# S5 input products of a hybrid decoder layer: split float32r operands stacked through DRAM, or plain float32 on four 32-row blocks

## The chip, the cores and the metric

The program runs on one NeuronCore of a Trainium2 chip. The metric is the time of one execution on the device in microseconds (us), the median of several runs. The engines are TensorE (PE; its weight loads are listed apart as PEld), VectorE (DVE), ScalarE (ACT), GpSimd (POOL) and SyncE (SP). Each works through its own instructions in the order in which the program lists them and waits on semaphores for the others.

## What is computed

One decoder layer on 256 positions of width 2048: RMSNorm, one wide projection, three mixing branches (gated MLP, S5 state-space model, stick-breaking attention), their gated sum, an output projection, and an MLP of 8192. The change is in the S5 branch. Its 1024 channels form 64 groups of 16, and each group drives 64 complex states:

```python
u = xin.astype(f32).reshape(bsz, seq, S5_GROUPS, S5_GROUP_CH)
bu_re = jnp.einsum('blgh,gph->blgp', u, bb_re)
bu_im = jnp.einsum('blgh,gph->blgp', u, bb_im)
_, _, s_re, s_im = lax.associative_scan(combine, (a_re, a_im, bu_re, bu_im), axis=1)
y = einsum('blgp,ghp->blgh', s_re, c_re) - einsum('blgp,ghp->blgh', s_im, c_im)
```

The input products are `bu_re` and `bu_im`. The kernel puts the factor that turns `b` into `bb` into the output weights instead, so the products use `b` as it is loaded.

## The kernel before

**The stream.** Almost all work is in large matmuls over weight blocks of 512 KB, numbered in the order in which they are used (`plan`): S5 input (blocks 0 to 15), q, k and v (16 to 63), the MLP branch's v and u (64 to 95), gates and branch outputs (96 to 223), the GLU (from 224), and so on. Each block is loaded into a `raw` tile by SP's queue (L195), cast to `hi` in float32r by ScalarE (L214), and the rest `lo` = raw - hi is taken by VectorE. `begin_unit(u)` loads five blocks ahead and converts three ahead; then PE does the block's matmuls with hi and lo (L289 and L293, or L351, L352 and L354, or L320, L321 and L328).

**The side work.** Everything else is in tasks, generators that `pump()` (L224) advances once after each block. A task that yields BAR goes on after the next block; a budget of VectorE time per block, which all tasks share, can end its turn earlier. New tasks go to the front of the list unless `front=False`. So attention and the gated MLP come ahead of S5 wherever both are ready, and a task that emits less VectorE work lets those behind it come earlier. The instructions of a task stand on each engine behind those of the block after which they were emitted.

**Side results.** Products of the tasks go to PSUM tiles `side(name)` (L141), from the pool `ps_sd` of four banks. A bank is free for a new tile when the last instruction that reads the old one is done. Attention uses two such tiles for each step of a pair of heads: `pz` (scores), `pc` (sums of logs), `pyc` (output). Their names carry the head: `pc6` and `pc7` belong to the pair whose other tiles are `za3`, `le3` and `sp3`. `le` takes the sums by an addition on VectorE and then an exponential on ScalarE (L882). The gated MLP's task `gmlp` (L911) opens with the row sums `rv_s` on VectorE, from the sums of squares `ssv` of `vg`.

**S5.** A half h is 128 channels, that is four row blocks of 32 channels with 128 states each; a chunk ch is half of it (two row blocks, j). `s5_split_b` (L513) loads `b` in two tiles, splits each into hi and lo and stores both in the DRAM tile `bd`; `s5_split_u` (L529) does the same with the S5 input `s5x` into `ud`. For each chunk `stack` (L653) reads back three pieces for each operand, so that 96 rows hold hi, lo, hi of `b` against hi, hi, lo of `u`: one float32r matmul over 96 rows then is the product. `bu_mm` (L668) does four of these a chunk into two side tiles `pb`, and `bu_evac` (L678) copies them to `bu` on ScalarE. Then VectorE rotates `bu` by a table `cs` (products `rt`, made from table products `tt`), scans, rotates back, and `y_mm` (L767) forms the output `py`, in float32, with eight matmuls on four blocks of columns. `s5_go` (L996) starts this when the preparation and the splits are done. Small tiles of 128x1024 float32 come from one pool of `NACT` = 32.

Of the kernel before, what the change touches and what calls it, by code (L numbers as in the profile page):

```python
# [17 lines left out]
P = 128  # L18
D = 2048
T = 256  # L20
# [7 lines left out]
NACT = 32  # L28
# [63 lines left out]
def hybrid_trunk(  # L92
# [31 lines left out]
    dram = ctx.enter_context(tc.tile_pool(name="dram", bufs=1, space=bass.MemoryType.DRAM))  # L124
# [384 lines left out]
    ud = dram.tile([P, MT, 2, T], F32R, name="ud")  # L509
    bd = dram.tile([P, MT, 2, 2 * P], F32R, name="bd")  # L510
    st = {}

    def s5_split_b():  # L513

        for i in range(2):
            br = a4([P, 4, 2 * P], F32, f"br{i}")
            S.dma_start(br, s5_b[:, 4 * i:4 * i + 4])
            yield BAR
            yield BAR
            hi = a4([P, 4, 2 * P], F32R, f"bh{i}")  # L520
            lo = a4([P, 4, 2 * P], F32R, f"bl{i}")
            S.copy(hi, br)
            V.tensor_sub(lo, br, hi.bitcast(F32))
            yield 1135
            yield BAR
            G.dma_start(bd[:, 4 * i:4 * i + 4, 0, :], hi)
            G.dma_start(bd[:, 4 * i:4 * i + 4, 1, :], lo)

    def s5_split_u(i):  # L529
        hi = a4([P, 4, T], F32R, f"uh{i}")  # L530
        lo = a4([P, 4, T], F32R, f"ul{i}")
        S.copy(hi, s5x[i])
        V.tensor_sub(lo, s5x[i], hi.bitcast(F32))
        yield 1135
        yield BAR
        G.dma_start(ud[:, 4 * i:4 * i + 4, 0, :], hi)
        G.dma_start(ud[:, 4 * i:4 * i + 4, 1, :], lo)
# [109 lines left out]
    def s5_run():  # L647
        mag, kre, kim, e1, e16, e128 = (st[n] for n in ("mag", "kre", "kim", "e1", "e16", "e128"))
        bu_of, cks, cts, st_of, bs_of, tab, py, pbs, tmp = {}, {}, {}, {}, {}, {}, {}, {}, {}
        bdv = bd.rearrange("(i p) h s c -> p h s i c", p=32)  # L650
        udv = ud.rearrange("(i p) h s c -> p h s i c", p=32)

        def stack(ch):  # L653

            h, c = divmod(ch, 2)
            bs = s5w.tile([P, 2, 2 * P], F32R, tag="bs", name=f"bs{ch}")
            su = s5w.tile([P, 2, T], F32R, tag="su", name=f"su{ch}")
            for blk in range(3):
                rows = slice(32 * blk, 32 * blk + 32)
                G.dma_start(bs[rows], bdv[:, h, blk % 2, 2 * c:2 * c + 2])  # L660
                G.dma_start(su[rows], udv[:, h, blk // 2, 2 * c:2 * c + 2])
            bs_of[ch], st_of[ch] = bs, su
            if c == 1:
                ct = s5w.tile([P, 2, 4, 32], F32, tag="ct", name=f"ct{h}", bufs=1)
                S.dma_start(ct, s5_c[:, h])
                cts[h] = ct
# [11 lines left out]
        def bu_evac(ch):  # L678
            bu = a4([P, 2, 2, T], F32, f"bu{ch}")
            for j, pb in enumerate(pbs.pop(ch)):  # L680
                S.copy(bu[:, :, j, :], pb.rearrange("p (r t) -> p r t", r=2))  # L681
            bu_of[ch] = bu
# [100 lines left out]
        stack(0)  # L783
        yield from table_a(0)
        yield BAR
        stack(1)
# [6 lines left out]
        for ch in range(16):  # L793
            yield BAR
            if ch + 2 < 16:
                stack(ch + 2)
            if ch + 1 < 16:
                bu_mm(ch + 1)
# [3 lines left out]
            if ch + 1 < 16:  # L802
                bu_evac(ch + 1)
# [165 lines left out]
    def do_proj(kind, i, us):  # L969
        dsts = {"s5": s5x, "q": qT, "k": kT, "u": uT}[kind]  # L970

        def ev(b, ps):
            if dsts[i] is None:
                dsts[i] = a4([P, 4, T], F32, f"{kind}{i}")
            dst = dsts[i]
            o = dst[:, 2 * b:2 * b + 2, :]
            V.tensor_mul(o, ps if kind == "s5" else wide_sum(ps, f"w{kind}{i}_{b}"), rb)
            if kind == "u":
                def act():
                    S.activation(o, o, AF.Gelu_apprx_tanh)  # L980
                    if i == 1 and b == 1:
                        gm["u"] = True

                later(1, act)
            if kind == "s5" and b == 1:
                spawn(f"su{i}", s5_split_u(i))
                if i == 1:
                    spawn("s5", s5_go(), front=False)

        if kind == "s5":  # L990
            run_T(us, xs, ev)
        else:
            for j, u in enumerate(us):
                run_W([(u, lambda ps, j=j: ev(j, ps))], xs)

    def s5_go():  # L996
        while any(n in ("s5p", "s5b", "su0", "su1") for n, _ in tasks):
            yield BAR
        for _ in range(3):
# [158 lines left out]
    for kind, arg, us in plan:  # L1158
        if kind == "s5" and arg == 0:
# [3 lines left out]
            def ev0(b, ps):  # L1163
                V.tensor_mul(s5x[0][:, 2 * b:2 * b + 2, :], ps, rb)
                if b == 1:
                    spawn("su0", s5_split_u(0))

            def mid0(i):
# [11 lines left out]
                if i == 7:  # L1180
                    spawn("s5b", s5_split_b(), front=False)
# [93 lines left out]
```

## Time and profile before

| | |
|---|---|
| median of 3 runs | 1545.67 us (1545.59 to 1545.78) |
| the profiled execution | 1545.78 us |
| its span, first to last instruction | 1544.1 us |
| PE busy | 1528.4 us, 99% |
| VectorE busy | 1097.1 us, 71% |
| ScalarE busy | 764.0 us, 49% |
| `pb` matmuls (L674) | 64 records |
| `py` matmuls (L772) | 128 records for 64 matmuls |

A row of the timeline gives the start from the beginning of the span, the time until the last of the row's instructions ends, the engine, the line, the operation, what is written and read, and how many instructions the row joins. Matmuls are pipelined: one that is listed with 390 ns may let the next start after 230, so costs in the stream of PE are read from starts. Square brackets hold the idle time ahead of the row and what ended it.

### The profile page before, as it was taken

To read this page: it belongs to the slowest core of one execution; us is meant where nothing else is said; L and a number is where in the kernel's file an instruction comes from. 1 tells how busy PE (TensorE), PEld (TensorE's weight loads), DVE (VectorE), ACT (ScalarE), POOL (GpSimd) and SP (SyncE) were. 2 spreads that over 40 slices of the span, in tenths; PEclk is the share of its full clock that TensorE was granted. 3 is DMA by queue.
4 is the path that set the end of the run, shared out by engine and by line. 5 is a ranking of instruction groups with operands and counts; after the bars stand their busy time and mean duration, and the time that the engine had idled before them with its cause. 6 is when DMAs were issued, how large, how long until landed. Compare 5 with 4: busy or idle time off the path is not lost.

```text
span 1544.1 us, 20755 instructions
## 1 busy us (share of the span) xinstructions
PE 1528.4 (99%) x7900; PEld 1303.8 (84%) x7900; DVE 1097.1 (71%) x1454; ACT 764.0 (49%) x947; POOL 67.3 (4%) x126
## 2 busy tenths in 40 slices
PE   9999999999999999999999999999999999999997
PEld 9988888888888888898888888888888888888886
DVE  6886988989999999967655665466545564556554
ACT  7546577555546555564444443344434444344442
POOL 0301021001001000000000000000000000000000
PEclk9999999999999999999999999999999999999999
DMA  9965565657666666656666555555555555555653
GB/s 342 328 199 164 186 211 172 197 175 225 202 212 212 199 215 200 192 177 209 205 202 194 188 189 193 196 187 188 192 195 191 188 188 193 195 190 187 219 194 105
DMA packets 97411, 308.67 MB, mean 200 GB/s; under 512 B 11296, under 2 KB 22560, under 8 KB 97312
## 3 DMA queue, kind: packets, MB, share of 16 engines
q1 hardware_dynamic: 79200, 285.25, 56.2%
q0 software_dynamic: 11904, 10.49, 3.2%
q10 hardware_dynamic: 6208, 11.61, 2.4%
q8 instruction: 62, 1.02, 0.3%
q14 instruction: 37, 0.30, 0.1%
HBM read 301.02 MB, written 6.29 MB: 199 GB/s over the span
## 4 chain that ended last, share of the span: by engine, by line
PE 96%; DVE 1%; issue 1%; ACT 1%; DMA 1%; SPq 0%; POOLq 0%; POOL 0%; DVEq 0%; ACTq 0%
PE mm L289 21%; PE mm L351 19%; PE mm L352 19%; PE mm L354 19%; PE mm L293 11%; PE mm L320 1%; PE mm L321 1%; PE mm L328 1%; PE py L772 1%; PE pb L674 0%; DMA raw<-in_w_in 0%; ACT hi L214 0%; DVE lo L86 0%; DMA raw<-in_w_m 0%; DVE x L86 0%
## 5 line engine op out<-in xcount | busy, mean ns | idle before, releaser
L86 DVE TENSOR_TENSOR lo<-raw,hi 128x1024 fp32r<-128x1024 f32 (+1 forms) x537 | 653.3, 1220 | 380.1 <-ACT hi L214 365.5
L214 ACT CAST hi<-raw 128x1024 fp32r<-128x1024 f32 (+1 forms) x537 | 561.4, 1049 | 634.7 <-PE mm L352 397.7
L289 PE MATMUL mm<-xz,hi 128*128 128x512 f32 x1024 | 256.5, 392 | 0.0
L289 PEld LDWEIGHTS mm<-xz,hi 128*128 128x128 f32 x1024 | 184.4, 189 | 33.2
L351 PE MATMUL mm<-hi,xs 128*128 128x512 f32 x512 | 200.8, 392 | 0.0
L352 PE MATMUL mm<-hi,xs 128*128 128x512 f32 x512 | 199.5, 390 | 0.0
L352 PE MATMUL mm<-hi,ff 128*128 128x512 f32 x480 | 186.8, 389 | 0.0
L351 PE MATMUL mm<-hi,ff 128*128 128x512 f32 x480 | 186.8, 389 | 0.0
L293 PEld LDWEIGHTS mm<-xz,lo 128*128 128x128 f32 x1024 | 139.7, 190 | 10.0
L293 PE MATMUL mm<-xz,lo 128*128 128x256 f32 x1024 | 142.8, 282 | 0.0
L354 PE MATMUL mm<-lo,xs 128*128 128x512 f32 x512 | 137.0, 389 | 0.0
L354 PE MATMUL mm<-lo,ff 128*128 128x512 f32 x480 | 128.3, 389 | 0.0
L351 PEld LDWEIGHTS mm<-hi,xs 128*128 128x128 f32 x512 | 96.1, 188 | 21.9 <-ACT bu L681 1.6
L354 PEld LDWEIGHTS mm<-lo,xs 128*128 128x128 f32 x512 | 96.1, 188 | 20.2
L352 PEld LDWEIGHTS mm<-hi,xs 128*128 128x128 f32 x512 | 96.2, 188 | 19.4
L352 PEld LDWEIGHTS mm<-hi,ff 128*128 128x128 f32 x480 | 90.1, 188 | 18.7
L354 PEld LDWEIGHTS mm<-lo,ff 128*128 128x128 f32 x480 | 90.1, 188 | 18.7
L351 PEld LDWEIGHTS mm<-hi,ff 128*128 128x128 f32 x480 | 90.1, 188 | 18.6
L289 PE MATMUL mm<-xs,hi 128*128 128x512 f32 x384 | 96.6, 393 | 0.3 <-DVE s5x L86 0.3
L289 PEld LDWEIGHTS mm<-xs,hi 128*128 128x128 f32 x384 | 69.1, 189 | 13.3 <-ACT hi L214 0.5
L86 DVE TENSOR_TENSOR rt<-bu,cs 128x1024 f32<-128x1024 f32 x64 | 76.8, 1221 | 0.3
L293 PEld LDWEIGHTS mm<-xs,lo 128*128 128x128 f32 x384 | 52.4, 190 | 3.8
(252 smaller groups left out, 1681.3 us busy)
## 6 DMA issues: line engine op xcount, KB each, us to landing
raw<-in_w_m SPq DMA_DIRECT2D x256, 512.0 KB, 4.3
raw<-in_w_in SPq DMA_DIRECT2D x143, 512.0 KB, 4.2
raw<-in_w_wide SPq DMA_DIRECT2D x48, 512.0 KB, 4.4
raw<-in_w_br SPq DMA_DIRECT2D x48, 512.0 KB, 4.3
raw<-in_w_out SPq DMA_DIRECT2D x32, 512.0 KB, 3.8
x<-in_x ACTq DMA_DIRECT2D x8, 512.0 KB, 5.8
raw<-in_w_glu SPq DMA_DIRECT2D x8, 512.0 KB, 4.3
bs<-bd POOLq DMA_DIRECT2D x48, 64.0 KB, 4.7
```

Of the source, the lines that this page charges most:

```text
L86: return fn(*a, **kw)
L214: S.copy(hi[:, k, :], raw[:, k, :])
L289: PE.matmul(pt[:, nb, :], lhsT=hi[:, k, nb * P:(nb + 1) * P], rhs=src.both(4 * i + k), start=4 * i + k == 0, stop=False)
L293: PE.matmul(pt[:, nb, T:], lhsT=lo[:, k, nb * P:(nb + 1) * P], rhs=src.hi(4 * i + k), start=False, stop=4 * i + k == last)
L320: PE.matmul(po, lhsT=wh, rhs=src.hi(kt), start=kt == 0 and nb % 2 == 0, stop=False)
L321: PE.matmul(po, lhsT=wh, rhs=src.lo(kt), start=False, stop=False)
L328: PE.matmul(po, lhsT=lo[:, k, nb * P:(nb + 1) * P], rhs=src.hi(kt), start=False, stop=kt == 2 * nk - 1 and nb % 2 == 1)
L351: PE.matmul(ps[tt], lhsT=xh, rhs=hi[:, k, :], start=kt == 0, stop=False)
L352: PE.matmul(ps[tt], lhsT=xl, rhs=hi[:, k, :], start=False, stop=False)
L354: PE.matmul(ps[tt], lhsT=xh, rhs=lo[:, k, :], start=False, stop=kt == 2 * nk - 1)
L772: PE.matmul(py[h][32 * i:32 * i + 32, :T], lhsT=cks[h][:, ri, i, :], rhs=s[i // 2][:, ri, i % 2, :], start=ri == 0, stop=ri == 1, tile_pos ...
```

## The change

The products are made in plain float32 from the tiles that are there, and the DRAM tiles, the splits and the stacking go. `b` is loaded once into two tiles that stay (`s5_load_b`). For a half, four row blocks i stand at partitions 32i to 32i + 31 of `s5x` and of `b`; each gets matmuls of its own at row position 32i of the array, into a side tile of its own, first the four for the real part, then the four for the imaginary part. So a whole half (two chunks) is done at once, every second chunk. `NACT` is 34, and `s5_go` waits for the preparation alone.

```diff
-NACT = 32
+NACT = 34
...
-        while any(n in ("s5p", "s5b", "su0", "su1") for n, _ in tasks):
-            yield BAR
-        for _ in range(3):
+        while any(n == "s5p" for n, _ in tasks):
             yield BAR
...
+    def s5_load_b():
+        for i in range(2):
+            t = a4([P, 4, 2 * P], F32, f"s5b{i}")
+            S.dma_start(t, s5_b[:, 4 * i:4 * i + 4])
+            s5bs.append(t)
...
-        def bu_mm(ch):
-            su, bs = st_of.pop(ch), bs_of.pop(ch)
-            pbs[ch] = []
-            for j in range(2):
-                pb = side(f"pb{ch}_{j}")
-                for ri in range(2):
-                    PE.matmul(pb[:, ri * T:(ri + 1) * T], lhsT=bs[0:96, j, ri * P:(ri + 1) * P],
-                              rhs=su[0:96, j, :], start=True, stop=True)
-                pbs[ch].append(pb)
+        def bu_mm(h):
+
+            pbs[h] = [side(f"pb{h}_{i}") for i in range(4)]
+            for ri in range(2):
+                for i in range(4):
+                    r = slice(32 * i, 32 * i + 32)
+                    PE.matmul(pbs[h][i][:, ri * T:(ri + 1) * T],
+                              lhsT=s5bs[h // 4][r, h % 4, ri * P:(ri + 1) * P],
+                              rhs=s5x[h // 4][r, h % 4, :], start=True, stop=True,
+                              tile_position=(32 * i, 0))
...
-            if ch + 2 < 16:
-                stack(ch + 2)
-            if ch + 1 < 16:
-                bu_mm(ch + 1)
+            if ch % 2 == 1 and ch < 15:
+                load_c(ch // 2 + 1)
+                bu_mm(ch // 2 + 1)
             if ch > 0 and ch % 2 == 0:
                 y_mm(ch // 2 - 1)
             yield BAR
-            if ch + 1 < 16:
-                bu_evac(ch + 1)
+            if ch % 2 == 1 and ch < 15:
+                bu_evac(ch // 2 + 1)
```

Because the budget of `pump()` is shared, the order of the side work changes too. Three places follow, as they stand on their engines. In these rows the number behind a tile's second underscore is the tile's own, a bracket names the engines that the instruction waits for, and line numbers below belong to the changed file (L839 there is L873 before, L640 is the new `bu_mm`).

PE behind block 79, before: the two `pc` of attention's last pair, then block 80.

```order
L873 MATMUL pc6_2639<-sp3_2550,ntri_119 128x256 [waits DVE_49,PE_49]
L875 MATMUL pc6_2639<-sp3_2550,nones_117 128x128
L876 MATMUL pc6_2639<-sp3_2550,ntri_119 128x128
L873 MATMUL pc7_2643<-sp3_2550,ntri_119 128x256 [waits PE_49]
L875 MATMUL pc7_2643<-sp3_2550,nones_117 128x128
L876 MATMUL pc7_2643<-sp3_2550,ntri_119 128x128
L289 MATMUL mm80_2656<-xs0_145,hi80_2583 128x512 [waits Activation_49]
```

The same place now, from `pc7` on:

```order
L839 MATMUL pc7_2586<-sp3_2493,ntri_117 128x256 [waits PE_49]
L841 MATMUL pc7_2586<-sp3_2493,nones_115 128x128
L842 MATMUL pc7_2586<-sp3_2493,ntri_117 128x128
L640 MATMUL pb2_0_2592<-s5x0_139,s5b0_428 128x256
L640 MATMUL pb2_1_2593<-s5x0_139,s5b0_428 128x256 [waits PE_49]
L640 MATMUL pb2_2_2594<-s5x0_139,s5b0_428 128x256 [waits DVE_49]
L640 MATMUL pb2_3_2595<-s5x0_139,s5b0_428 128x256 [waits DVE_49]
L640 MATMUL pb2_0_2592<-s5x0_139,s5b0_428 128x256
L640 MATMUL pb2_1_2593<-s5x0_139,s5b0_428 128x256
L640 MATMUL pb2_2_2594<-s5x0_139,s5b0_428 128x256
L640 MATMUL pb2_3_2595<-s5x0_139,s5b0_428 128x256
L288 MATMUL mm80_2604<-xs0_141,hi80_2528 128x512 [waits Activation_49]
```

The third group of products (half 2) has come between `pc7` and block 80, and two of its four tiles wait for VectorE.

VectorE at blocks 79 and 80 (lo82 and lo83 are converted three blocks ahead), before:

```order
L86 TENSOR_TENSOR lo82_2624<-raw82_2581,hi82_2623 128x1024 [waits DMAHW4_49,PE_49,Activation_49]
L86 TENSOR_TENSOR cu1_1_2648<-ct1_2132,s5_kre_961 128x256 [waits DVE_49]
L86 TENSOR_TENSOR cu2_1_2649<-ct1_2132,s5_kim_962 128x256
L86 TENSOR_TENSOR ck1_2647<-cu1_1_2648,cu2_1_2649 128x128 [waits DVE_49]
L86 SCALAR_TENSOR_TENSOR ck1_2647<-cu1_1_2648,cu2_1_2649 128x128
L86 SCALAR_TENSOR_TENSOR cs3_2462<-cs3_2462,s5_cs_758,td3_2554 128x128 x2
L86 TENSOR_TENSOR lo83_2660<-raw83_2601,hi83_2659 128x1024 [waits DMAHW5_49,PE_49,Activation_49]
L86 TENSOR_REDUCE rv_s_2685<-ssv_135 128x2 [waits Activation_49]
L86 TENSOR_SCALAR rv_s_2685<-rv_s_2685 128x2 [waits DVE_49]
L86 TENSOR_TENSOR le3_2517<-pc6_2639,za3_2516 128x384 [waits PE_49]
L86 TENSOR_TENSOR le3_2517<-pc7_2643,za3_2516 128x384 [waits PE_49]
```

And now:

```order
L86 TENSOR_TENSOR lo82_2567<-raw82_2526,hi82_2566 128x1024 [waits DMAHW4_49,PE_49,Activation_49]
L86 TENSOR_TENSOR lo83_2608<-raw83_2546,hi83_2607 128x1024 [waits DMAHW5_49,PE_49,Activation_49]
L86 TENSOR_REDUCE rv_s_2633<-ssv_133 128x2 [waits Activation_49]
L86 TENSOR_SCALAR rv_s_2633<-rv_s_2633 128x2 [waits DVE_49]
L86 TENSOR_TENSOR le3_2464<-pc6_2582,za3_2463 128x384 [waits PE_49]
L86 TENSOR_TENSOR le3_2464<-pc7_2586,za3_2463 128x384 [waits PE_49]
```

The S5 rows between lo82 and lo83 have moved to earlier blocks; the additions that read `pc6` and `pc7` stay behind lo83 and `rv_s`.

VectorE ahead of the first pair's additions to `le0` (blocks 45 and 46), before:

```order
L86 SCALAR_TENSOR_TENSOR sp0_1533<-za0_1501,le0_1502 128x768 [waits Pool_49]
L86 SCALAR_TENSOR_TENSOR za0_1501<-za0_1501,le0_1502 128x768 [waits DVE_49]
L86 TENSOR_TENSOR lo48_1624<-raw48_1537,hi48_1623 128x1024 [waits DMAHW6_49,PE_49,Activation_49]
L86 SCALAR_TENSOR_TENSOR cs0_1567<-cs0_1567,s5_cs_758,td0_1616 128x128 x4
L86 TENSOR_TENSOR lo49_1664<-raw49_1577,hi49_1663 128x1024 [waits DMAHW7_49,PE_49,Activation_49]
L86 TENSOR_TENSOR le0_1502<-pc0_1643,za0_1501 128x384 [waits DVE_49,PE_49]
L86 TENSOR_TENSOR le0_1502<-pc1_1647,za0_1501 128x384 [waits PE_49]
```

And now, behind `sp0`, `za0` and the first product `rt1`:

```order
L86 TENSOR_TENSOR rt2_1600<-bu0_1541,cs0_1385 128x1024
L86 TENSOR_TENSOR bu0_1541<-rt1_1599,rt2_1600 128x512 [waits DVE_49]
L86 TENSOR_TENSOR bu0_1541<-rt1_1599,rt2_1600 128x512
L86 TENSOR_TENSOR lo48_1608<-raw48_1547,hi48_1607 128x1024 [waits DMAHW7_49,PE_49,Activation_49]
L86 TENSOR_TENSOR tt1_1_1636<-e16_872,e1_871 128x256 [waits DVE_49]
L86 TENSOR_TENSOR tt2_1_1637<-e16_872,e1_871 128x256
L86 TENSOR_TENSOR tt1_1_1636<-e16_872,e1_871 128x256
L86 TENSOR_TENSOR tt2_1_1637<-e16_872,e1_871 128x256
L86 TENSOR_TENSOR cs1_1635<-tt1_1_1636,tt2_1_1637 128x2x128 [waits DVE_49]
L86 TENSOR_TENSOR cs1_1635<-tt1_1_1636,tt2_1_1637 128x2x128
L86 TENSOR_TENSOR lo49_1647<-raw49_1570,hi49_1646 128x1024 [waits DMAHW0_49,PE_49,Activation_49]
L86 TENSOR_TENSOR le0_1490<-pc0_1627,za0_1489 128x384 [waits PE_49]
```

The S5 chain starts some four blocks earlier (`pb0` stands behind block 41 instead of block 45), so the first rotation and the second table now stand between `sp0` and `le0`. The `pyc` of that pair, which need `le0`, stand behind block 48 instead of block 47.

## Rows read from the trace of the kernel before

**Rows 1.** The page, part 1: busy us of each engine, share of the span, instructions.
```profile
PE 1528.4 (99%) x7900; PEld 1303.8 (84%) x7900; DVE 1097.1 (71%) x1454; ACT 764.0 (49%) x947; POOL 67.3 (4%) x126
```
**Rows 2.** Waits of PE: us in total, times, longest us.
```profile
PE pc L873 <- DVE sp L86: 1.7, 1, 1.7
```
**Rows 3.** Timeline of ScalarE at hi of block 10: start us, us, engine, line, operation.
```profile
29.38 1.05 ACT L214 CAST hi<-raw 128x1024 fp32r<-128x1024 f32 x1 [0.83 <-DMA raw<-in_w_in]
```
**Rows 4.** Timeline of PE, first matmul of block 10.
```profile
36.29 0.28 PE L320 MATMUL mm<-xs,hi 128*128 128x256 f32 x1
```
**Rows 5.** Timeline of PE around a `pb` group that stands alone.
```profile
192.93 1.08 PE L354 MATMUL mm<-lo,xs 128*128 128x512 f32 x4
193.85 0.64 PE L674 MATMUL pb<-su,bs 96*128 96x256 f32 x4
194.32 0.40 PE L351 MATMUL mm<-hi,xs 128*128 128x512 f32 x1
```
**Rows 6.** Timeline of PE around a `py` group that stands alone.
```profile
660.13 1.07 PE L354 MATMUL mm<-lo,xs 128*128 128x512 f32 x4
661.13 1.07 PE L772 MATMUL py<-bu,ck 128*32 128x256 f32 x16
662.13 0.50 PE L351 MATMUL mm<-hi,xs 128*128 128x512 f32 x1
```
**Rows 7.** Timeline of PE behind block 79: `pc6` begins, block 80 begins.
```profile
250.86 0.59 PE L873 MATMUL pc<-sp,ntri 128*128 128x256 f32 x2
...
252.53 2.10 PE L289 MATMUL mm<-xs,hi 128*128 128x512 f32 x8
```
**Rows 8.** Timeline of ScalarE there: hi83, and the last sum of squares of `vg1`.
```profile
250.15 1.06 ACT L214 CAST hi<-raw 128x1024 fp32r<-128x1024 f32 x1 [1.67 <-DVE za L86]
...
255.26 0.18 ACT L391 ACTIVATION_READ_ACCUMULATOR mm<-vg 128x1 f32 x1
```
**Rows 9.** Timeline of VectorE there: `rv_s` and the additions to `le3`.
```profile
256.41 0.15 DVE L86 TENSOR_REDUCE rv_s<-ssv 128x2 f32<-128x4 f32 x1
...
256.67 1.01 DVE L86 TENSOR_TENSOR le<-pc,za 128x384 f32<-128x384 f32 x2
```
**Rows 10.** Timeline of PE at the first `pc` (behind block 45), and blocks 46 and 47.
```profile
141.01 0.70 PE L873 MATMUL pc<-sp,ntri 128*128 128x256 f32 x2 [1.73 <-DVE sp L86]
...
143.35 2.00 PE L289 MATMUL mm<-xs,hi 128*128 128x512 f32 x8
...
146.13 2.00 PE L289 MATMUL mm<-xs,hi 128*128 128x512 f32 x8
```
**Rows 11.** Timeline of VectorE ahead of it: the first table, and `sp0`.
```profile
135.41 1.42 DVE L86 TENSOR_TENSOR tt<-e,e 128x256 f32<-128x256 f32 x4
136.87 0.76 DVE L86 TENSOR_TENSOR cs<-tt,tt 128x256 f32<-128x256 f32 x2
...
140.00 0.95 DVE L86 SCALAR_TENSOR_TENSOR sp<-za,le 128x768 f32<-128x768 f32 x1
```
**Rows 12.** Timeline of ScalarE there: hi46, `le0`'s exponential, copies of `pb`.
```profile
133.20 1.03 ACT L214 CAST hi<-raw 128x1024 fp32r<-128x1024 f32 x1
...
146.28 1.28 ACT L882 ACT_TABLE_LOAD   x1 [5.45 <-DVE le L86]
147.57 0.85 ACT L882 ACTIVATE le<-le 128x768 f32<-128x768 f32 x1
148.32 1.06 ACT L681 COPY bu<-pb 128x512 f32<-128x512 f32 x2
```
**Rows 13.** The page, part 5, VectorE's products: count | busy us, mean ns | idle.
```profile
L86 DVE TENSOR_TENSOR rt<-bu,cs 128x1024 f32<-128x1024 f32 x64 | 76.8, 1221 | 0.3
```
**Rows 14.** Timeline of PE's weight loads in a `pb` group.
```profile
221.81 0.54 PEld L674 LDWEIGHTS pb<-su,bs 96*128 96x128 f32 x4
```
**Rows 15.** Windows behind the last matmul: length, busy us (instructions) of PE, PEld, DVE, ACT, POOL, granted clock, DMA share, GB/s.
```profile
1533.00:1537.00 4.00, 0.00 (x0) 0.00 (x0) 2.58 (x7) 0.51 (x2) 0.56 (x1) 1.00 0.23 87
1537.00:1539.00 2.00, 0.00 (x0) 0.00 (x0) 0.00 (x0) 0.00 (x0) 0.00 (x0) 0.66 1.04 321
```

More of the change, by code (lines that the diff above doesn't have):

```diff
@@ L123, in hybrid_trunk @@
     s5w = ctx.enter_context(tc.tile_pool(name="s5w", bufs=2))
-    dram = ctx.enter_context(tc.tile_pool(name="dram", bufs=1, space=bass.MemoryType.DRAM))
     ps_mm = ctx.enter_context(tc.tile_pool(name="ps_mm", bufs=2, space=bass.MemoryType.PSUM))
@@ L508, in hybrid_trunk @@
     gs = Split(env, MT, "gs")
-    ud = dram.tile([P, MT, 2, T], F32R, name="ud")
-    bd = dram.tile([P, MT, 2, 2 * P], F32R, name="bd")
     st = {}
-    def s5_split_b():
+    s5bs = []
+    def s5_load_b():
         for i in range(2):
-            br = a4([P, 4, 2 * P], F32, f"br{i}")
-            S.dma_start(br, s5_b[:, 4 * i:4 * i + 4])
-            yield BAR
[L519 to L537, printed above, removed]
+            t = a4([P, 4, 2 * P], F32, f"s5b{i}")
+            S.dma_start(t, s5_b[:, 4 * i:4 * i + 4])
+            s5bs.append(t)
     def dve_exp(dst, src, name):
@@ L648, in s5_run @@
         mag, kre, kim, e1, e16, e128 = (st[n] for n in ("mag", "kre", "kim", "e1", "e16", "e128"))
[L649 to L666, printed above, removed]
@@ L668, in bu_mm @@
-        def bu_mm(ch):
-            su, bs = st_of.pop(ch), bs_of.pop(ch)
-            pbs[ch] = []
-            for j in range(2):
-                pb = side(f"pb{ch}_{j}")
-                for ri in range(2):
-                    PE.matmul(pb[:, ri * T:(ri + 1) * T], lhsT=bs[0:96, j, ri * P:(ri + 1) * P],
-                              rhs=su[0:96, j, :], start=True, stop=True)
-                pbs[ch].append(pb)
[L678 to L682, printed above, removed]
+        bu_of, cks, cts, tab, py, pbs, tmp = {}, {}, {}, {}, {}, {}, {}
@@ new lines, in load_c @@
+        def load_c(h):
+            cts[h] = s5w.tile([P, 2, 4, 32], F32, tag="ct", name=f"ct{h}", bufs=1)
+            S.dma_start(cts[h], s5_c[:, h])
+        def bu_mm(h):
[7 more added lines that the diff above has]
+                              tile_position=(32 * i, 0))
@@ L684, in make_ck, with bu_evac @@
+        def bu_evac(h):
+            pb = pbs.pop(h)
+            for c in range(2):
+                bu = bu_of[2 * h + c] = a4([P, 2, 2, T], F32, f"bu{2 * h + c}")
+                for j in range(2):
+                    S.copy(bu[:, :, j, :], pb[2 * c + j].rearrange("p (r t) -> p r t", r=2))
         def make_ck(h):
@@ L781, in y_evac @@
             yield 0
-        stack(0)
+        load_c(0)
         yield from table_a(0)
         yield BAR
-        stack(1)
         table_b(0)
@@ L984, in ev @@
                 later(1, act)
[L985 to L988, printed above, removed]
+            if kind == "s5" and b == 1 and i == 1:
+                spawn("s5", s5_go(), front=False)
         if kind == "s5":
@@ L996, in s5_go @@
     def s5_go():
-        while any(n in ("s5p", "s5b", "su0", "su1") for n, _ in tasks):
-            yield BAR
-        for _ in range(3):
+        while any(n == "s5p" for n, _ in tasks):
             yield BAR
@@ L1164, in ev0 @@
                 V.tensor_mul(s5x[0][:, 2 * b:2 * b + 2, :], ps, rb)
-                if b == 1:
-                    spawn("su0", s5_split_u(0))
             def mid0(i):
@@ L1180, in mid0 @@
                 if i == 7:
-                    spawn("s5b", s5_split_b(), front=False)
+                    s5_load_b()
                     spawn("s5p", s5_prep(), front=False)
```

## The prediction

> **What bounds the kernel now.** Start with the busy times: TensorE (PE) is busy 1528.4 of 1544.1 us [rows 1], VectorE 1097.1, ScalarE 764.0. Next ask whether the rest of PE's time is waits: the longest in its list is one of `pc` on VectorE, 1.7 us [rows 2]; most of what is left lies behind its last matmul. So from the first weight block to the last the program is one stream of matmuls, and a change is worth what it adds to or takes from that stream: time that its own matmuls hold the array, and new waits of PE. The profiled execution took 1545.78 us (span 1544.1 plus 1.68 around it), 0.11 above the median of 1545.67; sums are made on the former and the 0.11 is taken off at the end. One run of this kernel tells 0.2% (3.1 us) from no change; that is the bound for the chances.
>
> **What the removed work gives back.** Four casts on ScalarE, four subtractions on VectorE and, on POOL's queue, eight stores to DRAM and 96 reads back fall away. PE waited for none of them. The casts of block 10 show the cover: hi is ready at 29.38 + 1.05 = 30.43 [rows 3], PE uses it at 36.29 [rows 4], 5.9 us later. The only load that comes earlier, `s5b1`, 0.5 MB beside `s5b0` on ScalarE's queue, starts near the same place and is covered by the same 5.9 us. I cost all of this at nothing.
>
> **What the matmuls cost in the stream.** A `pb` group of before (one chunk) is read from starts: the last of four lo matmuls starts at 192.93 + (1.08 - 0.39) = 193.62, the next thing 0.23 later; with `pb` the next block starts at 194.32 instead of 193.85 [rows 5]. So 0.47 us a chunk, 16 chunks: 7.5 us go.
>
> The new group (a half, two chunks) has eight float32 matmuls on four blocks of the array. No row shows blocks of rows, but `py` is the same count and size on four blocks of columns: 16 records for eight matmuls, two passes each. Undisturbed, the block behind it starts at 662.13, where 660.13 + 0.68 + 0.23 = 661.04 would have been normal [rows 6]: 1.09 us, four rounds of four passes at 0.22 and about 0.1 us of emptying on either side. I take that: 8 x 1.09 = 8.7, so +1.2 us. The nearest rows for the bounds: passes that stream like the float32r `pb`, 0.12 each, give 4 x 0.12 + 0.18 = 0.65 a group (5.2, -2.3 us); passes that do not overlap at all give 16 x 0.22 + 0.18 = 3.7 a group (29.6, +22.1 us).
>
> A rule to set beside this: the Trainium skill (TensorE: Matmul & The Clock Gate, "Measured speedup vs the span model") gives four row blocks 3.07 times the speed of one, not four times. By it 16 passes of 0.22 would take an estimated 1.15 us plus the emptying, and the sum would be about 2 us higher; no run here shows it yet.
>
> **The new wait.** Every new group takes four `side` tiles at once, and `side` has four banks. So PE can't start the group until every earlier side product is read out. In seven of the eight places that has long happened. At block 79 it hasn't: the order puts `pb2` right behind `pc6` and `pc7`, whose banks are freed by the two VectorE additions to `le3`, and these stand one block later, behind lo83 and `rv_s`. PE must wait for them before it can go on to block 80.
>
> When are they done? In the trace of before `pc6` starts at 250.86 and block 80 at 252.53 [rows 7]. `rv_s` needs the sums of squares of `vg1`, which ScalarE makes after hi83 (250.15), with a table load, until 255.26 + 0.18 = 255.44 [rows 8]. All of that stands before `pb2` in time and is unchanged. VectorE then needs 0.26 from `rv_s` to the additions and 1.01 for both [rows 9]; before, `rv_s` ran only at 256.41, because `ck1` and `cs3` stood ahead of lo83. Those have moved away from there, so `rv_s` starts at 255.5, the additions end near 256.3 and 256.8. Block 3 of `pb2` still has four passes in a row from then, 0.86, and 0.1 of emptying: block 80 starts at 257.75. Without the wait it would be 252.53 + 1.09 = 253.62. So +4.1 us; 5.0 if VectorE is as late as before, 3.3 if the sums come 0.8 earlier.
>
> The Trainium skill (TensorEngine Tiling (Array Packing), "Gotcha 1: PSUM Pressure") warns of just this: row blocks write to different banks and need more of them. It gives no price; the rows above do.
>
> **The old wait and its successor.** Before, `pc0` started at 141.01 after 1.73 us of idle time [rows 10], on `sp0`, which VectorE began at 140.00 [rows 11]. Now `pb0` stands four blocks earlier, so PE is free at 139.28 + 1.09 = 140.37. ScalarE has four copies of `pb0` (1.06 for two) ahead of hi46 (133.20), which comes 2.1 later [rows 12], and VectorE has lost the first table (1.42 + 0.76, 2.2) from this stretch [rows 11]: `sp0` comes at 139.9, `pc0` at 140.9, 0.55 lost. But the additions to `le0` now stand behind the first rotation: after `sp0` come `za0` (0.9), two products (1.22 long [rows 13], 1.14 apart), two halves (1.2), lo48 (1.14), six table products (2.2), lo49 (1.14) and the additions (1.0), until 150.75; then ScalarE's table load and exponential, 1.28 and 0.85 [rows 12], until 152.9. PE comes to `pyc0` after `pc` (1.7, as in [rows 7]) and three blocks of 2.78 [rows 10], at 151.0: 1.9 lost. Together 2.45 for 1.73, +0.7 us. Ends: -1.7 (no wait is left) and +2.7 (VectorE 2 us later).
>
> **Sum.** 1545.78 + 1.2 + 4.1 + 0.7 - 0.11 = 1551.7 us, 0.4% slower. Own range of this case: 1549.0 to 1554.0.
>
> **Rivals.**
> 1. *Weights load one after another.* Each pass has a load of 128 columns; four loads of `pb` take 0.54, the last one 0.19, so 0.117 apart [rows 14]. If those of four row blocks don't overlap, a group takes 16 x 0.117 + 0.18 = 2.05, eight take 16.4, +8.9 in place of +1.2: 1559.4 us. Against it: the loads of `py` overlap, 16 in one group of 1.09; but they have 32 columns, not 128. By the Trainium skill (TensorE: Matmul & The Clock Gate, "LDWEIGHTS (loading the stationary operand)") a load's time goes by its columns and not by its rows, so 32 rows would save nothing.
> 2. *Blocks don't run side by side* (the change doesn't do what it says): 3.7 a group, +22.1: 1572.6 us. Against it: `py` does.
> 3. *Not slower.* A pass on 32 rows holds the array only as long as a float32r pass. Its place is the eight `pb` groups: 0.65 each, -2.3 us, and the passes left behind the wait at block 79 shrink by 0.4: -2.3 + 3.7 + 0.7 gives 1547.8 us, within 0.2%. It decides from 0.75 us a group. For it: `pb` before streams at 0.12; against: `py` is float32 too and takes 0.22.
> 4. *The clock falls in the gap at block 79.* PE would stand still some 3.4 us there (`pb2_0` and `pb2_1` end near 253.0). The granted clock was 1.00 after the wait of 1.7 us and still 1.00 four us after the last matmul, and fell to 0.50 within the next slice, 0.66 on average [rows 15]. A gap of 3.4 lies between. If it falls, blocks of 2.8 us take 5.6 until it is back; for one block, 1554.5, for two, 1557.3. By the Trainium skill (TensorE: Matmul & The Clock Gate, "The HAM clock gate") idle time is what lowers this clock.
>
> **Chances.** Forecast 0.58, rival 1 0.17, rival 2 0.06, rival 3 0.08, rival 4 0.11. The range from 1548.0 to 1560.0 leaves out rival 2, half of rival 3 and the tails of the rest, about 0.18. Within 0.2% lie 0.06 of the forecast (its low end) and 0.06 of rival 3: same 0.12. Faster needs rival 3 and both waits gone as well: 0.02 of its 0.08. The rest is slower: 0.86.
>
> **What would show it.** `pb` should have 128 records (eight matmuls of two passes, eight times) in rounds of four 0.22 apart, and a lone group should move the next block by 1.09. PE's waits should name VectorE's `le` at `pb2`, near 3.5 us, just ahead of block 80, and about 1.8 at the first `pyc`; `pc0` should fall below 1 us. A `pb` group of 2 us means rival 1, 3.7 rival 2, 0.65 rival 3; a granted clock under 1.00 near 257 us rival 4. I am wrong if there is no wait at `pb2`, or if PE has waits in the stages after 300 us, where I expect none.

## The result and the profile after

The changed kernel takes 1554.05 us (median of 4 runs, 1553.62 to 1554.56); the kernel before took 1545.64 beside it. The ratio is 1.0053 (95% interval 1.0041 to 1.0065): 8.4 us slower. That is 2.4 us above the forecast of 1551.7, inside the range of 1548.0 to 1560.0 that the chances go by and 0.05 us above the forecast's own range, which ended at 1554.0. The profiled execution has a span of 1552.0 us, 7.9 more than before.

The page of the changed kernel, busy us of each engine, against [rows 1]:

```profile
PE 1535.1 (99%) x7964; PEld 1303.3 (84%) x7964; DVE 1093.9 (70%) x1450; ACT 760.8 (49%) x944; POOL 12.2 (1%) x22
```

VectorE and ScalarE lost a little over 3 us each and POOL the 104 issues of its transfers (126 instructions before, 22 now); PE has 6.7 us more. The waits of PE (us in total, times, longest), against [rows 2]:

```profile
PE pb L640 <- DVE le L86: 4.2, 1, 4.2
PE pyc L856 <- ACT le L848: 1.7, 1, 1.7
PE pwarm L466 <- POOL ones L451: 1.0, 1, 1.0
PE mm L319 <- ACT hi L213: 0.9, 2, 0.7
PE pc L839 <- DVE sp L86: 0.8, 2, 0.4
```

The two waits of the forecast lead the list. A group of products that stands alone, timeline of PE, against [rows 5, 6]:

```profile
348.09 1.07 PE L353 MATMUL mm<-lo,xs 128*128 128x512 f32 x4
349.08 1.15 PE L640 MATMUL pb<-s5x,s5b 32*128 32x256 f32 x16
350.16 0.50 PE L350 MATMUL mm<-hi,xs 128*128 128x512 f32 x1
350.50 0.39 PE L351 MATMUL mm<-hi,xs 128*128 128x512 f32 x1
```

The next block would have started at 348.09 + 0.68 + 0.23 = 349.00 and starts at 350.16: 1.16 us. Its second matmul then follows 0.34 us behind its first instead of 0.23, and the next few lose 0.03 more: 1.30 in all. Block 79, PE:

```profile
252.06 0.67 PE L839 MATMUL pc<-sp,ntri 128*128 128x256 f32 x2 [0.41 <-DVE sp L86]
...
253.98 0.70 PE L640 MATMUL pb<-s5x,s5b 32*128 32x256 f32 x4
258.85 2.53 PE L640 MATMUL pb<-s5x,s5b 32*128 32x256 f32 x12 [4.16 <-DVE le L86]
261.31 3.47 PE L288 MATMUL mm<-xs,hi 128*128 128x512 f32 x8
264.62 1.11 PE L292 MATMUL mm<-xs,lo 128*128 128x256 f32 x8
265.57 2.00 PE L288 MATMUL mm<-xs,hi 128*128 128x512 f32 x8
```

`pc6` begins at 252.06 and block 80 only at 261.31. Ordinarily that takes 1.67 us [rows 7] and a group's 1.16, so 9.25 - 2.83 = 6.4 us are lost, and block 80's hi matmuls then take 3.31 us from start to start where block 81's take 1.84. Who was late, ScalarE and VectorE there, against [rows 8, 9]:

```profile
252.67 1.05 ACT L213 CAST hi<-raw 128x1024 fp32r<-128x1024 f32 x1 [2.22 <-DMA raw<-in_w_wide]
...
257.76 0.19 ACT L390 ACTIVATION_READ_ACCUMULATOR mm<-vg 128x1 f32 x1
...
257.98 0.16 DVE L86 TENSOR_REDUCE rv_s<-ssv 128x2 f32<-128x4 f32 x1 [1.66 <-ACT mm L390]
...
258.24 1.01 DVE L86 TENSOR_TENSOR le<-pc,za 128x384 f32<-128x384 f32 x2
```

The chain is the one of the forecast, from hi83 by `ssv` and `rv_s` to the additions. And why block 80 was slow, windows of 5 us (length, busy us of PE, PEld, DVE, ACT, POOL, granted clock, DMA share, GB/s):

```profile
250.00:255.00 5.00, 4.28 (x24) 3.06 (x22) 4.97 (x5) 2.76 (x3) 0.00 (x0) 1.00 0.57 204
255.00:260.00 5.00, 1.15 (x9) 1.11 (x11) 3.30 (x7) 4.83 (x9) 0.70 (x1) 0.74 0.84 279
260.00:265.00 5.00, 5.00 (x23) 3.59 (x16) 2.22 (x3) 2.37 (x6) 0.00 (x0) 0.57 0.10 39
265.00:270.00 5.00, 5.00 (x31) 4.37 (x30) 4.10 (x7) 1.93 (x2) 0.00 (x0) 1.00 0.31 103
```

The clock was 1.00 when PE fell idle, went to its lower level (0.50, 1.2 GHz) in the second half of the gap and was back at 1.00 from 265 on: rival 4 happened on top of the forecast.

One more difference lies behind the last matmul. VectorE's last instruction (timeline), in the kernel before:

```profile
1535.92 0.48 DVE L86 TENSOR_SCALAR last<-last,r3r 128x512 f32<-128x512 f32 x1
```

and in the changed one:

```profile
1546.81 0.48 DVE L86 TENSOR_SCALAR last<-last,r3r 128x512 f32<-128x512 f32 x1
```

SyncE's waits behind it, before:

```profile
SPq L1271 <- PEq L1271: 3.4, 2, 2.9
```

and now, where SyncE waits for the output transfer itself:

```profile
SPq L1231 <- DMA out<-last: 2.9, 1, 2.9
SPq L1231 <- PEq L1231: 0.6, 2, 0.4
```

The last VectorE instruction comes 10.9 us later than before, the end only 7.9 later. Before, 8.2 us lay between it and the end (1544.1), now 5.2 (1552.0). SyncE waited 2.9 us in the program's closing barrier (the view names PE's sequencer, but a barrier ends with its last engine). POOL's final drain, its instruction ahead of the barrier (the trace has a record of it that no view lists), says which: 9.18 us before, until 1543.28, and 0.66 now. So the stream lost 10.9 us and the end gave 3.0 back.

### The profile page after: what moved, and what is told of

The parts are those of the page before. It is cut to its first block, busy times and chain, and to the rows that moved or that the text cites. A ratio compares the mean times of both kernels' runs of the same rounds, so it can differ in the third digit from the quotient of the medians.

```text
span 1552.0 us, 20699 instructions
## 1 busy us (share of the span) xinstructions
PE 1535.1 (99%) x7964; PEld 1303.3 (84%) x7964; DVE 1093.9 (70%) x1450; ACT 760.8 (49%) x944; POOL 12.2 (1%) x22
## 4 chain that ended last, share of the span: by engine, by line
PE 93%; DVE 2%; ACT 2%; DMA 1%; issue 1%; SPq 0%; ACTq 0%; POOLq 0%; POOL 0%; DVEq 0%
PE mm L288 20%; PE mm L350 19%; PE mm L351 19%; PE mm L353 19%; PE mm L292 10%; PE mm L319 1%; PE mm L327 1%; PE mm L320 1%; DVE lo L86 1%; ACT hi L213 1%; PE pb L640 1%; PE py L740 1%; DMA raw<-in_w_wide 0%; DMA raw<-in_w_in 0%; DVE x L86 0%
```

## The experiments

**Run 1, hold.** The theory: the loss sits at block 79, in the wait and in the clock behind it. `pairs[0]` is set when attention emits `pc` and falls two blocks after the pair's output is read.

```diff
             if ch % 2 == 1 and ch < 15:
+                while pairs[0] or slot[0] < pairs[1]:
+                    yield BAR
                 load_c(ch // 2 + 1)
                 bu_mm(ch // 2 + 1)
...
```

> The changed kernel, but half 2's products wait until attention's last pair has read its side tiles: they then stand behind block 84 instead of between pc7 and block 80. Theory (the loss sits at block 79: a wait of 4.2 us for le plus some 2.5 us of half clock behind it): block 80 starts 1.7 us after pc6, no granted clock under 1.00 near 257 us; the lone group still costs 1.3 us, and pyc6, now behind block 81, waits some 0.85 us for the exponential of le. Sum -6.9 us against 1554.05: 1547.1, between 1546.3 and 1548. Rival A (the loss is the price of all eight groups, the wait at block 79 covers work that is needed anyway): within 0.5 of 1554.0. Rival B (the four banks are missing at the new place too, the wait only moves): 1549 to 1553, with a new wait of pb2 in PE's list.

Measured: 1547.19 us (1546.45 to 1547.48), 6.9 less than the changed kernel; against before 1.0008 (0.9999 to 1.0017). Timeline of PE at block 79 and at the new place of half 2:

```profile
251.46 0.67 PE L844 MATMUL pc<-sp,ntri 128*128 128x256 f32 x2 [0.43 <-DVE sp L86]
...
253.21 2.09 PE L288 MATMUL mm<-xs,hi 128*128 128x512 f32 x8
...
269.43 1.15 PE L640 MATMUL pb<-s5x,s5b 32*128 32x256 f32 x16
270.50 2.11 PE L288 MATMUL mm<-xs,hi 128*128 128x512 f32 x8
```

`pc6` to block 80 is 1.75 us, the granted clock stays at 1.00 from 250 to 265, and the group at its new place waits for nothing. Rivals A and B fall.

**Run 2, fill.** It parts the clock from the wait: PE gets something to do in the gap.

```diff
                 for i in range(4):
+                    if (h, ri, i) == (2, 0, 2):
+                        for _ in range(8):
+                            PE.matmul(pbs[h][0][:, T:], lhsT=ntri, rhs=rbc, start=True, stop=True)
                     r = slice(32 * i, 32 * i + 32)
```

> The changed kernel, with eight more float32 matmuls (128 rows, 256 columns, some 0.43 us each) put into the gap at block 79, between the second and the third block of rows of half 2, into a bank that is free and is written over afterwards; its output is not changed. They last some 3.45 us of a gap of 4.2, so the wait for le ends no later. Theory (the clock fell because PE stood still, and the fall costs 1.05 us in the rest of pb2 and 1.47 in block 80): the granted clock stays at 1.00 near 257 us and the time falls by 2.5 us to 1551.5 (1551 to 1552). Rival A (the clock falls all the same, or block 80 was slow for another reason): 1554.0. Rival B (the matmuls outlast the gap): a wait of PE on le of 0 and more than 1554.

Measured: 1551.73 us (1551.18 to 1551.98), 2.3 less than the changed kernel. Timeline of PE:

```profile
254.23 3.72 PE L641 MATMUL pb<-rbc,ntri 128*128 128x256 f32 x16
258.33 1.59 PE L643 MATMUL pb<-s5x,s5b 32*128 32x256 f32 x12 [0.38 <-DVE le L86]
259.85 2.14 PE L288 MATMUL mm<-xs,hi 128*128 128x512 f32 x8
261.83 1.10 PE L292 MATMUL mm<-xs,lo 128*128 128x256 f32 x8
```

and windows (columns as above):

```profile
255.00:260.00 5.00, 4.62 (x27) 3.39 (x26) 3.44 (x7) 4.83 (x9) 0.70 (x1) 1.00 0.81 293
260.00:265.00 5.00, 5.00 (x28) 4.29 (x29) 3.59 (x5) 2.85 (x6) 0.00 (x0) 1.00 0.04 12
```

The clock stays at 1.00. The rest of `pb2` takes 1.52 us instead of 2.46, block 80's hi part 1.98 instead of 3.31: 2.27 together, which is the 2.3 of the times. More work made the kernel faster. The Trainium skill (TensorE: Matmul & The Clock Gate, "HAM oscillation — how this bites in real kernels") says that idle stretches between bursts lower this clock; the trace agrees, with a gap of 4.16 us in one kernel and 0.38 in the other.

**Runs 3 and 7, the end.** Run 3 adds one transfer on POOL's queue to the changed kernel (`G.dma_start(one, s5_par[:, 0, :])` ahead of the loads of `b`), run 7 adds 104 tiny ones.

> The changed kernel with a single load of 16 KB (a copy of parameters that nothing reads) issued on POOL's queue beside the loads of b. Theory (a program that has used POOL's DMA queue ends with a long drain of POOL, 9.18 us in the kernel before against 0.66 in the changed one, so that the change gained 3.0 us behind the last matmul): the stretch from VectorE's last instruction to the end grows by 2.7 to 3.0 us and the time to 1556.9 (1556.5 to 1557.3). Rival A (the end of the kernel before was longer for another reason, its count of instructions or stores): 1554.0. Rival B (the drain grows with the number of transfers, 104 before against one here): 1554.0 to 1554.5.

Measured: 1554.42 us (1554.26 to 1554.74). No long end: the theory of a fixed price falls. But the record of the final drain grew from 656 to 745 ns, which is rival B and gives run 7 its number.

```diff
...
+                one = cst([P, NPAIR], "one")
+                for r in range(104):
+                    G.dma_start(one[r:r + 1], s5_par[r:r + 1, 0, :])
```

> The changed kernel with 104 tiny loads (128 bytes each, nothing reads them) issued on POOL's queue late in the program, where POOL has nothing else to do. Theory (the final drain grows with the number of transfers, some 85 ns each): the drain takes 9.2 to 9.8 us as in the kernel before, and the time grows by 2.8 to 3.3 us to 1557 (1556.5 to 1557.6). Rival (it grows with packets or bytes, 11904 packets and 10.49 MB in the kernel before): 104 packets add nothing, 1554.0.

Measured: 1568.26 us (1567.13 to 1569.85), far above 1557, but the end is as forecast. Waits of SyncE at the end:

```profile
SPq L1235 <- PEq L1235: 3.4, 2, 3.0
```

The final drain takes 9.164 us for 104 transfers of 128 bytes (3328 packets on POOL's queue in all): (9164 - 656) / 104 = 82 ns a transfer, the same as for the 104 large ones of before (11904 packets, 10.49 MB), (9179 - 656) / 104 = 82. So it goes by transfers, not by packets or bytes. The rest of the time is an accident of this run: the 104 issues ran from the program's start, from 1.68 us on, not late as I had meant, and POOL came to `r_r` (roots of row sums, which PE's early product `prow` needs by way of `diag`) at 52.16 us instead of 40.52. PE waits for that once:

```profile
PE prow L501 <- DVE diag L86: 9.2, 1, 9.2
```

By 57 us the stream is 10.6 us behind the changed kernel's, and at VectorE's last instruction (1558.17) 11.4.

**Run 4, order.** The loops of the products are swapped.

```diff
-            for ri in range(2):
-                for i in range(4):
+            for i in range(4):
+                for ri in range(2):
```

> The changed kernel with the loops of the products swapped: both matmuls (four passes) of one block of rows one after another, then the next block. Theory (passes overlap only with neighbours in the order that stand on other blocks of rows): only the last pass of a block runs beside the first of the next, so a group takes 13 passes in a row of 0.216 us, 2.8, plus 0.4 around it, instead of 1.3: +1.8 us in each of seven places and some +1 at block 79, 1567.5 (1564 to 1570). Rival (each block of rows works off its own passes, whatever their order, so that all four end together): a group still takes 1.3 and the time is 1554 (1553.5 to 1555).

Measured: 1554.72 us (1554.32 to 1554.91). My theory falls by 13 us, the rival holds. Timeline of PE at the same group as above:

```profile
348.88 1.07 PE L353 MATMUL mm<-lo,xs 128*128 128x512 f32 x4
349.88 1.17 PE L640 MATMUL pb<-s5x,s5b 32*128 32x256 f32 x16
350.98 0.50 PE L350 MATMUL mm<-hi,xs 128*128 128x512 f32 x1
```

Block to block this is 1.19 us (350.98 against 348.88 + 0.68 + 0.23), as with the other order. The edit did change the order on the engine: the first four matmuls of a group, one for each block of rows, start 13 ns apart, where they started 7 ns apart. Each block of rows works off its own passes while the others do theirs; the order within a group hardly matters. The Trainium skill (TensorEngine Tiling (Array Packing), "Key Properties") says that tiles load and multiply independently, and this run agrees (1.19 us against 1.16). The 0.7 us that the kernel is slower lie at block 79 alone: hi83 comes 0.24 us later there (252.91), and the clock comes back later (0.64 on average from 265 to 266 us, where the other order had 1.00).

**Run 5, old products without POOL.** The kernel before with all 104 transfers on ScalarE's queue (`S.dma_start` for `G.dma_start`; the DRAM tiles are typed float32 for it, the bytes are the same).

> The kernel before, with its eight stores to DRAM and 96 reads back issued on ScalarE's queue instead of POOL's; nothing else differs. One POOL transfer left the time of the changed kernel alone, but its final drain of POOL grew from 656 to 745 ns. Theory (the final drain grows by some 85 ns for each transfer that POOL issued: 104 of them make 9.2 us, which end 2.8 us after everything else): without them the time falls by 2.8 us to 1542.9 (1542.4 to 1543.5). Rival A (issuing costs ScalarE 0.33 us each, as the row of ct shows, 34 us in all, and the casts of hi come late behind six issues in a row): PE gets waits on hi, 1544 to 1550. Rival B (the end of the kernel before was long for another reason): 1545.7.

Measured: 1554.77 us (1552.05 to 1556.23). It is slower as in rival A, but beyond its range, and the waits are not the ones on `hi` that it named. The end does shrink (from VectorE's last instruction, 1547.02, to the end, 1552.2, it is 5.2 us, and the drain 0.66), but the stream loses 11.1. Waits of PE:

```profile
PE mm L289 <- DVE s5x L86: 4.1, 1, 4.1
PE pc L873 <- DVE sp L86: 1.7, 1, 1.7
PE pyc L890 <- ACT le L882: 1.4, 1, 1.4
```

New waits on ScalarE's and VectorE's products stand in the list; the clock fell behind the first (0.70 on average from 55 to 60 us). I followed only the first of them: ScalarE's copy for the split of `b` waits 4.95 us for its load, and VectorE behind it. That load now stands behind two stores of the split on the same queue and lands 10.8 us after its issue, where the slower of the two took 7.3 before; whether the queue or the traffic delays it was not tried. The rest of the loss comes in small steps in later blocks and was not taken apart. The Trainium skill (DMA: Bandwidth & Descriptors, "Issuing engine by pattern") calls transfers that SyncE or ScalarE issues generally faster; the reads back agree (`bs` lands 4.0 us after its issue on ScalarE's queue, 4.7 on POOL's). The kernel was slower all the same: in the part that was followed, work that the stream needs stands on ScalarE behind a transfer that came late.

**Run 6, hold and one block more.** Attention's `pc` and `pyc` each come one block later.

```diff
             yield 1700
             yield BAR
+            yield BAR
...
             yield 1000
             yield BAR
+            yield BAR
             v = vN[hb // 2]
```

> The changed kernel, with half 2's products held back from attention's side tiles as in the first run, and attention's pc and pyc one block later each, so that sp and the exponential of le are ready. Theory (what is left beside the groups are waits of PE on attention's operands: 2.2 us at two pyc and 0.9 at two pc): 1547.2 - 3.1 = 1544.1 (1543.5 to 1544.8), 1.6 below the kernel before. Rival (side tiles are held longer, so that the products of a half wait for banks at another place): 1546 to 1551 with a wait of pb in PE's list.

Measured: 1542.34 us (1542.1 to 1542.75); against before 0.9977 (0.9968 to 0.9987), faster than both kernels. Waits of PE, all of them:

```profile
PE pwarm L466 <- POOL ones L451: 1.0, 1, 1.0
PE mm L319 <- ACT hi L213: 0.7, 2, 0.4
```

No side product waits any more. The gain on run 1 is 4.9 us, not 3.1: read from the starts of the blocks, each of the four waits had cost 0.2 to 0.3 us more than the list says (the first `pc` 0.74 for 0.4, the first `pyc` 1.94 for 1.7): 4.0 us. The two profiled executions differ by just that, 1546.45 against 1542.48; most of the other 0.9 is that run 1's profiled execution was the fastest of its ten, 0.7 below their median. The hold itself has nothing left to do here: with attention later, half 2 comes at block 78, ahead of `pc6`.

**Run 8, twice.** Every group of products a second time, right behind the first, in run 1's kernel (`for ri in (0, 1, 0, 1)`).

> The held kernel of the first run with every group of products done twice, one right behind the other into the same banks (64 more matmuls of the same form, the output stays). Theory (a group is rounds of 0.216 us, four passes at a time, plus 0.44 us on its edges that is paid once): four more rounds in each of eight groups, 8 x 0.865 = +6.9 us, 1554.1 (1553.5 to 1554.7). Rival A (the edges are paid by every set of matmuls): 8 x 1.31 = +10.5, 1557.7. Rival B (the passes fit between the loads and cost little): under +4, below 1551.

Measured: 1552.2 us (1551.79 to 1552.47), +5.0. Timeline of PE at one group:

```profile
344.33 1.07 PE L353 MATMUL mm<-lo,xs 128*128 128x512 f32 x4
345.33 2.01 PE L640 MATMUL pb<-s5x,s5b 32*128 32x256 f32 x32
347.27 0.50 PE L350 MATMUL mm<-hi,xs 128*128 128x512 f32 x1
```

From 345.33 to 347.27 is 1.94 us, where run 1 had 1.07: +0.87 for four rounds, as the theory says, with the edges paid once. The step is the same in all eight places, 6.9 in all; what is missing to it is mostly found in the waits of `pc` and `pyc`, which list 1.9 us where run 1 has 3.1: PE comes later and waits less. The other way about, time saved ahead of such a wait would not show.

**Run 9, by chunks.** Two blocks of rows at a time, 16 groups.

```diff
-            pbs[h] = [side(f"pb{h}_{i}") for i in range(4)]
+            h, c = divmod(ch, 2)
+            pbs[ch] = [side(f"pb{ch}_{j}") for j in range(2)]
...
-                for i in range(4):
+                for j in range(2):
+                    i = 2 * c + j
...
```

> The changed kernel with the products done by chunks, two blocks of rows at a time, as often as before the change (16 groups of 8 passes instead of 8 of 16). Only two banks are taken at once, so there is no wait for le at block 79. Theory (a round takes 0.216 us however many blocks of rows are busy in it, and a group has 0.44 us on its edges): 16 x 1.31 instead of 8 x 1.31, +10.5 on 1546.6 (the held run less its 0.5 at pyc6): 1557.1; where seven groups stand beside a py the edges may be shared, 0.3 each, so 1554.5 to 1557.5. Rival (with half of the blocks idle a pass goes through in half the time): a group of 0.87, 16 x 0.87 = 13.9, +3.4: 1550.0 (1549 to 1551).

Measured: 1551.67 us (1551.07 to 1552.18). Timeline of PE at a lone group of two blocks:

```profile
522.57 1.07 PE L353 MATMUL mm<-lo,xs 128*128 128x512 f32 x4
523.57 1.13 PE L641 MATMUL pb<-s5x,s5b 32*128 32x256 f32 x8
524.63 0.50 PE L350 MATMUL mm<-hi,xs 128*128 128x512 f32 x1
```

1.15 us from block to block (524.63 against 522.57 + 0.68 + 0.23), with half of the passes: rounds cost 0.216 us however many blocks of rows take part, so the rival's group of 0.87 falls. The time is lower than either of the theory's sums because the new order has none of run 1's waits on attention (4.0 us by run 6): 4.5 + 4.0 = 8.5 for eight more groups, 1.06 each, most of them beside a `py`, whose edges they share. Read from starts, `pb` and `py` together cost 2.38 us there, and `py` alone 1.31. At block 79 the group takes two banks and waits for nothing.

**Run 10, old products, ScalarE's queue, attention later.** Run 5 with run 6's two lines.

> The kernel before, with its transfers on ScalarE's queue as in the fifth run and attention's pc and pyc one block later each. It asks whether the old products keep their price and lose both the long end and the wait of pc on sp. If the fifth run gives 1542.9, the 1.7 us at the first pc goes as well: 1541.2 (1540.7 to 1542). Rival (casts are late behind ScalarE's issues): PE waits on hi and the time is 1543 or more. Rival B (the wait of pc only moves to pyc or to another block): as the fifth run.

Measured: 1551.16 us (1550.14 to 1553.05). The wait of `pc` has gone, 3.4 us on `s5x` stay: the first rival's time, with the wait of run 5 in place of one on `hi`.

**Runs 11 and 12, old products, attention later.** Run 11 has only run 6's two lines on the kernel before; run 12 also reads the stacked operands back for a half at a time.

```diff
...
-            bs = s5w.tile([P, 2, 2 * P], F32R, tag="bs", name=f"bs{ch}")
-            su = s5w.tile([P, 2, T], F32R, tag="su", name=f"su{ch}")
+            bs = s5w.tile([P, 4, 2 * P], F32R, tag="bs", name=f"bs{h}", bufs=1)
+            su = s5w.tile([P, 4, T], F32R, tag="su", name=f"su{h}", bufs=1)
...
-                G.dma_start(bs[rows], bdv[:, h, blk % 2, 2 * c:2 * c + 2])
-                G.dma_start(su[rows], udv[:, h, blk // 2, 2 * c:2 * c + 2])
+                G.dma_start(bs[rows], bdv[:, h, blk % 2])
+                G.dma_start(su[rows], udv[:, h, blk // 2])
...
```

> The kernel before with attention's pc and pyc one block later each, so that both ways of making the products are compared in a stream without waits on attention. Theory (the 1.7 us that the first pc waits for sp go, nothing else changes): 1545.7 - 1.7 = 1544.0 (1543.3 to 1544.4); against the sixth run (1542.3) the row blocks would then be 1.7 us the cheaper way, 3.0 saved at the end less 0.35 more in each of some four halves. Rival A (the wait only moves): 1545.5. Rival B (the later attention collides with the next products): above 1546.

> As the eleventh run, with the stacked operands read back for a half at a time: 48 reads on POOL's queue instead of 96, so 56 transfers in all instead of 104; the matmuls stay as they are. Theory (POOL's final drain takes 0.66 us and some 82 ns for each transfer): 0.66 + 56 x 0.082 = 5.2 us, so that it ends at 1539.3 on the clock of the kernel before, ahead of SyncE (1540.55), and the last 2.8 us go: 1544.0 - 2.8 = 1541.2 (1540.5 to 1542), below every kernel so far. Rival A (the drain grows with bytes, which stay): no gain, as the eleventh run. Rival B (with one buffer instead of two a half's operands come late): PE waits at pb, above 1544.

Measured: run 11 1543.86 us (1543.46 to 1547.07; against before 0.9987, 0.9978 to 0.9996), run 12 1540.95 us (1540.75 to 1541.31; 0.9968, 0.9956 to 0.998). Run 12 is the fastest kernel of the study. SyncE's waits at its end:

```profile
SPq L1273 <- DMA out<-x: 2.2, 1, 2.2
SPq L1273 <- PEq L1273: 0.7, 2, 0.5
```

The barrier's 3.4 us are 0.7. The final drain takes 5.257 us for 56 transfers, (5257 - 656) / 56 = 82 ns each again, though the bytes are those of before. Run 6 against run 11 is the change compared like with like: the stream of the row blocks is 1.4 us longer (VectorE's last instruction at 1535.35 against 1533.98), the end 3.0 shorter, and the time 1.5 lower. They were not timed side by side, and taken each against the kernel before that ran beside it the gain is 1.1; the traces, 1.4 less 3.0, say 1.6.

## Why the prediction was right where it was, and where not

- **Removed work, costed at nothing.** Wrong at the end, and by a little in the stream. "PE waited for none of them" looks only at PE's stream: POOL's drain waits for nothing that the stream sees, and 104 x 82 ns of it outlasted everything else by 3.0 us. The forecast is too high by that. Nor was it quite so in the stream. The list of [rows 2] has a short wait at block 16 that is gone from the list now:

```profile
PE mm L289 <- DVE s5x L86: 0.3, 1, 0.3
```

  In the trace of before, `s5x` stands on VectorE behind a subtraction of the split of `b` (1.22 us at 48.23), with no idle time between. Block 16 gains 0.5 us by the starts of its matmuls, and 1.0 between runs 11 and 6.
- **Groups, +1.2.** The mechanism is right: 128 records, rounds of four passes 0.216 apart, loads of 128 columns overlapped. The next block starts 1.16 us late, forecast 1.09. Mis-sized is the price as such: I read it from the start of the next block, and a tiled group still holds back that block's second matmul, here (0.34 for 0.23) as in the `py` group of [rows 6], whose follower's second matmul starts at 662.47, 0.34 behind the first. The old `pb` group has no such tail ([rows 5]; its follower's second matmul comes at 194.55, 0.23 behind). So a half costs 1.30 for 0.94, +0.36: 2.9 us in eight groups that stand alone. Start by start of the same blocks, the changed stream falls back by 0.35 us a half from 300 us on, which makes 2.8 for eight. Runs 6 and 11 show the same; their 1.4 at the end is 2.8 less 1.0 at block 16 and 0.4 in the first 10 us. The sum "about 2 us higher" that the prediction set beside its own came near in size, but the blocks do run at four times the speed of one: a round of four passes costs 0.216 us (run 8), no more than one pass of the full array (16 in 3.72 us in run 2), and the loss is on the edges.
- **The wait at block 79, +4.1.** Right in place, chain and cause; run 1 takes it away and run 9 does without it. Measured: 9.25 us from `pc6` to block 80, less 2.83, less the clock's 0.94 in the rest of `pb2`, 5.5 us. The step that failed is "all of that stands before `pb2` in time and is unchanged": hi83 came 0.61 us behind the start of `pc6`, where it had come 0.71 ahead of it [rows 7, 8], 1.3 us later, because its block was loaded late. The trace shows two steps more. The load started at 248.89 (246.08 before), just when VectorE had read block 79 out of the buffer that it needs (`NRAW` is 4; lo79 ends at 248.86, before at 246.06). And hi79, which lo79 needs, stands on ScalarE behind the activations of attention's last pair, which began 4 us later, first before, then now:

```profile
237.50 0.84 ACT L861 ACTIVATE le<-za 128x768 f32<-128x768 f32 x1
...
241.49 0.85 ACT L827 ACTIVATE le<-za 128x768 f32<-128x768 f32 x1 [1.51 <-POOL za L822]
```

  So, by the trace, the new order of the side work moved the chain that the prediction held fixed; no run tried this.
- **Old wait and successor, +0.7.** Right: `pc0` 0.41 us, the first `pyc` 1.7, forecast under 1 and 1.8. A second `pc` (`pc6`, 0.4) was not foreseen, and waits cost 0.2 to 0.3 us each beyond the list (run 6).
- **Rival 4, the clock, given 0.11.** It came true together with the forecast and cost 2.3 us (run 2), for a gap of 4.16 us instead of the 3.4 that I had put in. Counting it as another case instead of adding its share was wrong: with a gap between 1.7 us, which was harmless, and four, I had no row that spoke for 1.00.
- **Rivals 1 to 3** fall by the rows of the lone group: 1.16 us from block to block, not 2.05, 3.7 or 0.65.

The parts make 5.5 + 2.3 + 2.8 + 1.0 (the other waits, by starts) - 0.7 (the first 55 us) = 10.9 in the stream, as measured, less 3.0 at the end. That the forecast's 6.0 came so close was partly luck: the clock (2.3), the later chain (1.4), the groups' edges (1.6) and 0.3 of waits were missing on one side, and the end (3.0) and the first 55 us (0.7) on the other.

## What to carry to other kernels

Before an instruction that takes several banks at once is put behind others, ask in which place the last reader of each bank stands in its engine's order; here one misplaced group cost nearly 8 us, and giving attention's operands one block more (run 11) was worth some 2 us, more than the change itself gains in a stream free of attention's waits (1.1 to 1.6). When PE must stand still for some us, price the lower clock behind the gap as part of the wait. And count what an engine still has to close at the end of the program: fewer, larger transfers on POOL's queue (run 12) gave 2.9 us without touching a matmul.

## What the hardware showed that I had not expected

- The final drain of POOL grows by some 82 ns for each transfer that it issued, whatever its size or its number of packets: 0.656 us for none, 0.745 for one, 5.257 for 56 (11136 packets), 9.164 for 104 (3328 packets) and 9.179 for 104 (11904).
- Passes on different blocks of rows overlap whatever the order in which the program lists them (1.19 us against 1.16 a group), and a group of two blocks takes as long as one of four (1.15).
- A tiled group costs 0.43 us on its edges beside its rounds, part of it inside the block that follows.
- In the gap of 4.16 us the clock fell, and it stayed at the lower level for nearly 7 us, more than 5 of them with PE at work again from 258.85 (windows of 1 us: 0.72 from 257 to 258, 0.50 to 264, 0.87 to 265); behind the gap of 1.7 us of the kernel before it stayed at 1.00 (windows of 2 us from 139 to 147).
